# Where the modulation's products are computed: a third of layer 0 moves from TensorE to VectorE, ScalarE and GpSimd, layer 1's loads move to GpSimd's queue

## The chip, the cores and the metric

The kernel runs on one core of a Trainium2 chip. A core has a tensor engine (PE, with its weight loads listed apart as PEld), VectorE (DVE), ScalarE (ACT), GpSimd (POOL) and SyncE (SP), each with an instruction stream of its own that it executes in order. An engine waits for another through semaphores. SP, ACT and POOL can issue DMA transfers; the page lists SP's and ACT's transfers as hardware queues and POOL's as a software queue (q0). The metric is the device time of one execution in microseconds.

## What is computed

Two transformer blocks follow each other on 256 tokens of width 1024, all in fp32. The first block has a gated delta rule, a dilated attention, an output product and a SwiGLU FFN with a short convolution. The second block has two layers with attention and a mixture of 16 experts, and both layers are modulated by a vector c. The change concerns only the modulation:

```python
silu_c = jax.nn.silu(c)
for i in range(DEPTH_2):                       # 2 layers
    mod = silu_c @ ada_w[i] + ada_b[i]         # 1024 x 6144 each
    sh1, sc1, g1, sh2, sc2, g2 = [m[:, None, :] for m in jnp.split(mod, 6, axis=-1)]
    h = rms_norm(x, norm_mix_g[i]) * (1.0 + sc1) + sh1
    ...                                        # attention, y
    x = x + g1 * y
    h = rms_norm(x, norm_ffn_g[i]) * (1.0 + sc2) + sh2
    x = x + g2 * grouped_moe(h, ...)
```

The modulation depends on c and its weights alone, so it can be computed at any time before the second block.

## The kernel before

The first block runs to about 412 us, the second from there to the end. In the first block PE multiplies weights and activations that are each split into a high and a low part (names ending in h and l): ACT makes the high part of a weight block (wh, or whl for both parts in one tile), DVE, sometimes POOL, the low part (wl). `subs` does this for the blocks of one 1 MB load, `feat` multiplies them into features (L572), and lines L588 to L590 into tokens. The FFN has 22 steps (NFF); each has two `feat` blocks, a gate on ACT and DVE (L1109 to L1113), and the product back (L1096 to L1098) for the step before.

The modulation's two weight matrices are 48 MB. The kernel handles them as 48 units of 1 MB, in order, `ada_unit(n)`: units 0 to 23 are layer 0, 24 to 47 layer 1. `ada(n)` adds to a due count and issues the units that are due. It is called by `fill`, which the delta rule and the attention call where PE would wait, and once in each FFN step with a constant `step`; the due counts are the same before and after. Each unit loads a tile `wa` (128 x 2048); there are two such tiles, so a load waits until the unit two before has been read.

- Layer 0, `ada_rows(s, k)`: the tile is a block of 128 rows (k) by 2048 columns (s). PE multiplies it by one column of silu(c), spread over 32 columns: four products of 128 x 512 go to four strips of 32 rows of one PSUM tile (L401). After eight blocks (k = 7) the gate columns get their bias by products with the identity (L409), ACT copies the row out (`adarow`, L412) and sends it to DRAM (`adar`).
- Layer 1: a tile holds four blocks of 128 rows for one slice of 512 columns, and two units (u = 0, 1) make a slice. DVE scales the first block into `acc` (L382) and adds six others by SCALAR_TENSOR_TENSOR (STT, L387), with these exceptions: blocks 3 and 7 are scaled by ACT in place (L384) and added by POOL (L385). `ada_sum` then adds up the 128 partitions of `acc` by products with ones on PE (L422) and, for gate columns, the bias (L425). It runs two slices later.

All loads of both kinds are issued by SP (L396 and L375), in one queue with the weights of the first block. The values come back from `adar` by POOL's loads `adat` and `g`, which also issues the attention tables (`nb`, `rel`, `reld`). The second norm of the first block stands between the output product (`w_out`) and the FFN: ACT squares, POOL takes the root (`rs`, L500), DVE scales (`xn`, L502), PE transposes (L510), ACT and DVE split the result into `hh` and `hl`; some products whose results are not used (L470) run on PE meanwhile. A scheduler of the tile framework arranges each engine's instructions from the order in which the code is written.

The kernel begins with five products of ones (L268), which nothing uses.

Of the kernel before, what the change touches and what calls it, by code (L numbers as in the profile page):

```python
# [13 lines left out]
AF = mybir.ActivationFunctionType  # L14
ALU = mybir.AluOpType
# [78 lines left out]
def _pack(inp):  # L94
    g = {k: np.asarray(v) for k, v in inp.items()}
    A = np.ascontiguousarray

    def cols(v):
        return np.asarray(v).reshape(-1, 128).T

    def feat(w):

        n = w.shape[1]
        return A(w.reshape(KD, 128, n // 256, 2, 128).transpose(2, 1, 3, 0, 4)).reshape(n // 256, 128, 2048)

    def tok(w):

        n = w.shape[1]
        return A(w.reshape(2, 4, 128, n // 512, 512).transpose(3, 0, 2, 1, 4)).reshape(n // 256, 128, 2048)

    o = {"x": A(g["x"][0])}
    prm = np.zeros((128, NPRM), np.float32)
    for name, v in (("ln1", cols(g["ln1"][0])), ("ln2", cols(g["ln2"][0])),
                    ("conv", g["conv_qkv"][0].reshape(4, 12, 128).transpose(2, 1, 0).reshape(128, 48)),
                    ("fconv", g["ffn_conv"][0].reshape(3, 22, 128).transpose(2, 1, 0).reshape(128, 66)),
                    ("gdn", cols(g["gdn_norm"][0])), ("nmix", cols(g["norm_mix_g_2"])),
                    ("nffn", cols(g["norm_ffn_g_2"])), ("c", cols(g["c_2"][0])),
                    ("aqg", np.tile(g["a_q_gain_2"][0], 2)[:, None]), ("akg", np.tile(g["a_k_gain_2"][0], 2)[:, None]),
                    ("asub", g["a_subln_g_2"][0][:, None]),
                    ("bqg", np.tile(g["b_q_gain_2"][0], 2)[:, None]), ("bkg", np.tile(g["b_k_gain_2"][0], 2)[:, None]),  # L120
                    ("adab", cols(g["ada_b_2"]))):
        prm[:, PRM[name][0]:PRM[name][1]] = v
    o["prm"] = prm
    o["row"] = np.concatenate([g["a_log"][0], g["dt_bias"][0], g["router_bias_2"],
                               g["a_lambda_2"][0].ravel()])[None].astype(np.float32)
    o["lnf"] = A(g["ln_f"][None])
    w = g["w_in"][0]
    o["w_qkv"] = feat(w[:, 0:1536])
    o["w_z"] = tok(w[:, 1536:2048])
    o["w_qk"] = feat(w[:, 2056:3080])  # L130
    o["w_v"] = tok(w[:, 3080:3592])
    o["w_ba"] = A(w[:, 2048:2056].reshape(8, 128, 8).transpose(1, 0, 2)).reshape(128, 64)
    o["w_out"] = tok(g["w_out"][0])
    gu = np.stack([g["w_gate"][0].reshape(D, NFF, 128), g["w_up"][0].reshape(D, NFF, 128)], axis=2)
    o["w_gu"] = feat(gu.reshape(D, 2 * NFF * 128))
    o["w_dn"] = A(g["w_down"][0].reshape(11, 2, 128, D).transpose(0, 2, 1, 3)).reshape(11, 128, 2048)

    o["ada_p"] = A(g["ada_w_2"][0].reshape(8, 128, 3, 2048).transpose(2, 0, 1, 3)).reshape(24, 128, 2048)
    o["ada_w"] = A(g["ada_w_2"][1].reshape(2, 4, 128, 12, 512).transpose(3, 0, 2, 1, 4)).reshape(24, 128, 2048)
    o["t5"] = A(g["t5_bias_2"])  # L140
    for p in "ab":
        o[p + "_qkv"] = tok(g[p + "_w_qkv_2"][0])
        o[p + "_wo"] = tok(g[p + "_w_o_2"][0])
    o["rel"] = A(np.pad(g["b_rel_bias_2"][0], ((0, 0), (0, 127)))[:, 383::-1])
    rw = np.zeros((128, 8, 32), np.float32)
    rw[:, :, :16] = g["router_w_2"].reshape(8, 128, 16).transpose(1, 0, 2)
    o["rw"] = rw.reshape(128, 256)
    gu = np.empty((2, 8, 8, 128, 2, 2, 512), np.float32)
    for i, n in enumerate(("moe_w_gate_2", "moe_w_up_2")):
        gu[:, :, :, :, :, i] = g[n].reshape(2, 8, 2, 8, 128, 512).transpose(0, 1, 3, 4, 2, 5)  # L150
    o["m_gu"] = gu.reshape(16, 8, 128, 2048)
    md = g["moe_w_down_2"].reshape(2, 8, 2, 4, 128, D)
    md = md.reshape(2, 8, 2, 2, 2, 128, 2, 512).transpose(0, 1, 6, 3, 5, 2, 4, 7)
    o["m_dn"] = A(md).reshape(16, 4, 128, 2048)
    o["cst"], o["dil"], o["hot"] = _constants()
    return o
# [14 lines left out]
def tile_block(ctx: ExitStack, tc: tile.TileContext, a: dict, out: bass.AP, dbg=None):  # L171
    nc = tc.nc
# [6 lines left out]
    pa = ctx.enter_context(tc.tile_pool(name="pa", bufs=4, space=PSUM))  # L179
# [3 lines left out]
    mm = nc.tensor.matmul  # L183
    V, G, A_ = nc.vector, nc.gpsimd, nc.scalar
# [14 lines left out]
    def w2(shape, name, dt=F32):  # L199
        return act.tile([128] + shape, dt, tag="w2", name=name, bufs=10)  # L200
# [7 lines left out]
    def ps(n=512, tag="pb"):  # L208
        p = pa if tag == "pa" else pb
        return p.tile([128, n], F32, tag=tag, name=tag)  # L210
# [53 lines left out]
    ones = const.tile([128, 128], F32, name="ones")  # L264
    V.memset(ones, 1.0)

    for _ in range(5):
        mm(ps(512, "pa"), ones, ones[:, 0:1].to_broadcast([128, 512]), start=True, stop=True)  # L268
    mhalf = const.tile([128, 8], F32, name="mhalf")
    G.memset(mhalf, -0.5)  # L270
    epsc = const.tile([128, 1], F32, name="epsc")
# [92 lines left out]

    csil = const.tile([128, 8], F32, name="csil")
    adar = [dr.tile([6 * D], F32, name=f"adar{l}") for l in range(2)]
    ada_acc, ada_sums = [None], []

    def ada_unit(n):

        if n < 24:
            return ada_rows(n // 8, n % 8)
        l, s, u = n // 24, n // 2 % 12, n % 2
        w = adap.tile([128, 2048], F32, tag="wa", name="wa", bufs=2)
        nc.sync.dma_start(w, a["ada_w"][n - 24])  # L375
        if u == 0:
            ada_acc[0] = adap.tile([128, 512], F32, tag="acc", name="acc", bufs=3)
        acc = ada_acc[0]
        for i in range(4):
            wi, k = w[:, i * 512:(i + 1) * 512], 4 * u + i  # L380
            if k == 0:
                V.tensor_scalar(acc, wi, csil[:, k:k + 1], None, op0=ALU.mult)  # L382
            elif i == 3:
                A_.activation(wi, wi, AF.Copy, scale=csil[:, k:k + 1])  # L384
                G.tensor_tensor(acc, acc, wi, op=ALU.add)  # L385
            else:
                V.scalar_tensor_tensor(acc, wi, csil[:, k:k + 1], acc, op0=ALU.mult, op1=ALU.add)  # L387
        if u == 1:
            if len(ada_sums) == 2:
                ada_sums.pop(0)()  # L390
            ada_sums.append(lambda: ada_sum(l, s, acc))

    def ada_rows(s, k):

        w = adap.tile([128, 2048], F32, tag="wa", name="wa", bufs=2)
        nc.sync.dma_start(w, a["ada_p"][8 * s + k])  # L396
        if k == 0:
            ada_acc[0] = ps(512, "pa")
        p = ada_acc[0]
        for j in range(4):  # L400
            mm(p[32 * j:32 * j + 32, :], csil[:, k:k + 1].to_broadcast([128, 32]), w[:, j * 512:(j + 1) * 512],  # L401
               start=(k == 0), stop=(k == KD - 1 and (4 * s + j) // 2 not in (2, 5)))
        if k < KD - 1:
            return
        for c in range(4):
            for j in range(4):
                if (4 * s + j) // 2 in (2, 5):
                    n = 16 * s + 4 * j + c
                    mm(p[32 * j:32 * j + 32, c * 128:(c + 1) * 128], P("adab")[:, n:n + 1].to_broadcast([128, 32]), ident,  # L409
                       start=False, stop=(c == 3))  # L410
# [349 lines left out]
    n = 0  # L760
# [64 lines left out]
    for u in range(6):  # L825
        for j, (wh, wl) in enumerate(subs(a["w_qkv"][u] if u else first_)):
            f = 2 * u + j
            p = ps(256, "pa")
            feat(p, hh, wh, wl)
            o = qkvT[f // 4][:, f % 4]  # L830
# [915 lines left out]
```

## Time and profile before

| | us |
|---|---|
| median of 3 runs | 1127.56 |
| lowest, highest | 1124.36, 1133.11 |
| the profiled execution | 1134.06 |
| its span, first to last instruction | 1132.4 |
| PE busy | 1084.4 (96%) |
| DVE busy | 588.6 (52%) |
| ACT busy | 444.1 (39%) |
| POOL busy | 151.8 (13%) |

The shares are averages over stages that have different limits, so the rows below cut the span into stretches. A profile shows one execution: how an engine was busy, what ended each idle time ("idle before, <- releaser"), and when a transfer was issued. When a transfer landed is seen from what began after it.

### The profile page before, as it was taken

What the parts mean: (1) busy time and instruction counts of PE and PEld (TensorE: products, weight loads), DVE (VectorE), ACT (ScalarE), POOL (GpSimd) and SP (SyncE); (2) the same over time, 40 slices, a digit from 0 to 9 for tenths busy, and PEclk for the clock granted to TensorE, in tenths of its full rate; (3) what the DMA queues carried; (4) which work ended last, traced back from release to release, by engine and by line L of the source; (5) the groups of instructions that cost most, each with busy time, mean ns of one, the idle gap of its engine ahead of it and who ended that gap; (6) DMA issues with size and microseconds to landing.
All of it is one profiled execution on the core that took longest, in us unless ns stands there. A gap on an engine that the chain in (4) does not pass through costs nothing. (4 is left out here: it accounts for less than half of the span.)

```text
span 1132.4 us, 16818 instructions
## 1 busy us (share of the span) xinstructions
PE 1084.4 (96%) x6524; PEld 702.4 (62%) x6524; DVE 588.6 (52%) x1215; ACT 444.1 (39%) x901; POOL 151.8 (13%) x126
## 2 busy tenths in 40 slices
PE   8999999999999989999999999898999999999898
PEld 6967666799998868778434343435887634443432
DVE  6954345798998766677412121226667722221212
ACT  5752254655554556667211011216555511110200
POOL 1223112131322241101000000004121000000000
PEclk9999999999999999999999999999999999999999
DMA  8586769878887855455999899999665699989995
GB/s 334 222 290 240 274 243 292 301 262 331 302 338 258 333 227 181 149 179 194 348 401 404 331 424 418 420 420 403 194 197 183 221 406 368 424 337 420 421 422 242
DMA packets 56463, 349.71 MB, mean 309 GB/s; under 512 B 6740, under 2 KB 7492, under 8 KB 19512
## 3 DMA queue, kind: packets, MB, share of 16 engines
q1 hardware_dynamic: 53744, 342.51, 78.0%
q0 software_dynamic: 1792, 5.62, 1.9%
q8 instruction: 54, 0.88, 0.3%
q10 hardware_dynamic: 840, 0.43, 0.1%
q14 instruction: 33, 0.27, 0.1%
HBM read 347.40 MB, written 1.14 MB: 308 GB/s over the span
## 5 line engine op out<-in xcount | busy, mean ns | idle before, releaser
L234 ACT CAST wh<-w 128x1024 fp32r<-128x1024 f32 x132 | 137.6, 1043 | 95.6 <-PE pa L589 67.3
L234 DVE TENSOR_TENSOR wl<-w,wh 128x1024 fp32r<-128x1024 f32 x110 | 136.4, 1242 | 59.3 <-ACT wh L234 46.3
L1578 PE MATMUL pb<-w,XT 128*64 128x512 f32 x672 | 151.8, 595 | 3.7 <-ACTq L1538 3.7
L1578 PEld LDWEIGHTS pb<-w,XT 128*64 128x64 f32 x672 | 47.7, 137 | 91.1 <-issue 81.9
L588 PE MATMUL pa<-wh,hh 128*128 128x512 f32 x224 | 91.0, 408 | 2.5 <-ACT hh L561 2.5
L589 PE MATMUL pa<-wh,hl 128*128 128x512 f32 x224 | 89.2, 398 | 3.0 <-POOL hl L559 1.7
L1597 DVE TENSOR_TENSOR he<-he,pb 128x512 f32<-128x512 f32 (+1 forms) x20 | 11.4, 580 | 154.0 <-PE pb L1578 100.0
L590 PE MATMUL pa<-wl,hh 128*128 128x512 f32 x224 | 88.9, 397 | 0.0
L234 POOL TENSOR_TENSOR wl<-w,wh 128x1024 fp32r<-128x1024 f32 x22 | 53.0, 2407 | 247.6 <-ACT wh L234 206.3
L1615 PE MATMUL pb<-w,heT 128*64 128x512 f32 x352 | 81.0, 603 | 1.5 <-ACT heT L224 1.5
L1596 ACT ACTIVATE he<-pb 128x512 f32<-128x512 f32 (+1 forms) x20 | 10.1, 513 | 184.2 <-PE pb L1578 184.2
L1578 PE MATMUL pb<-wx,XT 128*64 128x512 f32 x352 | 80.2, 595 | 0.0
L1618 DVE SCALAR_TENSOR_TENSOR he<-pb,gsl,g 128x512 f32<-128x512 f32 x32 | 24.1, 752 | 100.3 <-PE pb L1615 100.2
L572 PE MATMUL pb<-hh,whl 128*128 128x256 f32 x320 | 61.9, 286 | 0.0
L234 ACT CAST yh<-he 128x512 fp32r<-128x512 f32 x30 | 18.5, 616 | 107.0 <-DVE he L1618 107.0
L385 POOL TENSOR_TENSOR acc<-acc,wa 128x512 f32<-128x512 f32 x24 | 40.8, 1699 | 134.0 <-DVE acc L387 74.0
L1615 PEld LDWEIGHTS pb<-w,heT 128*64 128x64 f32 x352 | 24.6, 140 | 49.7 <-issue 45.8
L1578 PEld LDWEIGHTS pb<-wx,XT 128*64 128x64 f32 x352 | 25.9, 137 | 46.4 <-issue 45.4
L572 PE MATMUL pb<-hh,wh 128*128 128x256 f32 x192 | 54.4, 284 | 0.0
L572 PE MATMUL pb<-hl,wh 128*128 128x256 f32 x192 | 54.3, 283 | 0.0
L572 PE MATMUL pb<-hh,wl 128*128 128x256 f32 x192 | 54.3, 283 | 0.0
L572 PEld LDWEIGHTS pb<-hh,whl 128*128 128x128 f32 x320 | 51.2, 191 | 2.4 <-issue 1.4
(450 smaller groups left out, 2340.9 us busy)
## 6 DMA issues: line engine op xcount, KB each, us to landing
w<-in_m_gu SPq DMA_DIRECT2D x84, 1024.0 KB
w<-in_m_dn SPq DMA_DIRECT2D x42, 1024.0 KB
wa<-in_ada_p SPq DMA_DIRECT2D x24, 1024.0 KB
wa<-in_ada_w SPq DMA_DIRECT2D x24, 1024.0 KB
wx<-in_m_gu SPq DMA_DIRECT2D x48, 512.0 KB
w<-in_w_gu SPq DMA_DIRECT2D x22, 1024.0 KB
wx<-in_m_gu SPq DMA_DIRECT2D x20, 1024.0 KB
w<-in_a_qkv SPq DMA_DIRECT2D x12, 1024.0 KB
```

The source lines that it names most:

```text
L234: return A_.copy(h, i), (eng or V).tensor_tensor(l, i, h.bitcast(F32), op=ALU.subtract)
L385: G.tensor_tensor(acc, acc, wi, op=ALU.add)
L572: mm(p, w[:, c], r[:, k, :], start=(n == 0), stop=(n == 3 * KD - 1))
L588: mm(p[b], hh_, wh[:, c], start=(k == k0), stop=False)
L589: mm(p[b], hl_, wh[:, c], start=False, stop=False)
L590: mm(p[b], hh_, wl[:, c], start=False, stop=((k + 1) % KD == k0))
L1578: mm(pu[i][64 * e:64 * e + 64, :], xt[k // 4][:, k % 4, c0 + 64 * e:c0 + 64 * e + 64], w(e, i), start=(k == 0), stop=(k == KD - 1))
L1596: A_.activation(he[:, cs], pu[0][:, cs], AF.Silu)
L1597: V.tensor_tensor(he[:, cs], he[:, cs], pu[1][:, cs], op=ALU.mult)
L1615: pin(mm(pd[h][64 * e:64 * e + 64, :], heT[:, k, e, :], w(e, i), start=(k == 0), stop=(k == 3)))
L1618: V.scalar_tensor_tensor(he, pd[h], gsl, g2[:, h * 512:(h + 1) * 512], op0=ALU.mult, op1=ALU.mult)
```

## The change

Layer 0's units with n % 3 == 2 (8 of 24, their columns are 4096 to 6143) go the way of layer 1, through SP's queue; the other 16 stay with `ada_rows`. The arrays are cut accordingly (`ada_p` 16 tiles, `ada_w` 32). Layer 1's loads are issued by POOL (`nc.gpsimd`). In the way of layer 1, block 0 is scaled into `acc` by ACT, blocks 1 to 6 are added by DVE, and block 7 is scaled by ACT into a tile `last` of its own, which POOL adds: one POOL add for each slice where there were two, and DVE has six STT where it had a scaling and five STT. The products at the start are 12 of 216 columns. Lines behind the change stand five further down (L422 becomes L427).

```diff
-    for _ in range(5):
-        mm(ps(512, "pa"), ones, ones[:, 0:1].to_broadcast([128, 512]), start=True, stop=True)
+    for _ in range(12):
+        mm(ps(216, "pa"), ones, ones[:, 0:1].to_broadcast([128, 216]), start=True, stop=True)
...
+        if n < 24 and n % 3 < 2:
+            n = n // 3 * 2 + n % 3
+            return ada_rows(n // 8, n % 8)
         if n < 24:
-            return ada_rows(n // 8, n % 8)
+            n = 16 + n // 3
         l, s, u = n // 24, n // 2 % 12, n % 2
         w = adap.tile([128, 2048], F32, tag="wa", name="wa", bufs=2)
-        nc.sync.dma_start(w, a["ada_w"][n - 24])
+        (nc.gpsimd if l else nc.sync).dma_start(w, a["ada_w"][n - 16])
...
             if k == 0:
-                V.tensor_scalar(acc, wi, csil[:, k:k + 1], None, op0=ALU.mult)
-            elif i == 3:
-                A_.activation(wi, wi, AF.Copy, scale=csil[:, k:k + 1])
-                G.tensor_tensor(acc, acc, wi, op=ALU.add)
+                A_.activation(acc, wi, AF.Copy, scale=csil[:, k:k + 1])
+            elif k == 7:
+                last = w2([512], "last")
+                A_.activation(last, wi, AF.Copy, scale=csil[:, k:k + 1])
+                G.tensor_tensor(acc, acc, last, op=ALU.add)
             else:
                 V.scalar_tensor_tensor(acc, wi, csil[:, k:k + 1], acc, op0=ALU.mult, op1=ALU.add)
...
         if k == 0:
-            ada_acc[0] = ps(512, "pa")
-        p = ada_acc[0]
+            ada_pacc[0] = ps(512, "pa")
+        p = ada_pacc[0]
```

PE before, from the end of the output product (L590) over the second norm to the FFN's first products (L572); `wa,csil` are the modulation's products, `ident,prm` the gate bias, `ident,x` the unused products, `ident,xn` the transposes:

```order
L590 MATMUL pa<-wl,yh 128x512
L401 MATMUL pa<-wa,csil 32x512
L470 MATMUL pa<-ident,x 16x384 x4
L510 MATMUL pb<-ident,xn 128x128 x16
L401 MATMUL pa<-wa,csil 32x512 x7
L409 MATMUL pa<-ident,prm 32x128 x8
L572 MATMUL pb<-hh,wh 128x256
```

PE with the change, in the same place:

```order
L595 MATMUL pa<-wl,yh 128x512
L406 MATMUL pa<-wa,csil 32x512 x3
L414 MATMUL pa<-ident,prm 32x128
L475 MATMUL pa<-ident,x 16x384 x4
L414 MATMUL pa<-ident,prm 32x128 x7
L515 MATMUL pb<-ident,xn 128x128 x16
L577 MATMUL pb<-hh,wh 128x256
```

The products behind the transposes now stand ahead of them; 22 units of four products stood ahead of this place before, 15 and a quarter do now.

POOL before, from the second norm (`rs`) into the FFN:

```order
L234 TENSOR_TENSOR wl<-w,wh 128x1024
L500 TENSOR_TENSOR rs<-rs,mhalf 128x1 x2
L234 TENSOR_TENSOR wl<-w,wh 128x1024
L385 TENSOR_TENSOR acc<-acc,wa 128x512 x3
L1126 DMA rel<-in_rel 16x384
```

POOL with the change, in the same place:

```order
L235 TENSOR_TENSOR wl<-w,wh 128x1024
L379 DMA wa<-in_ada_w 128x2048
L505 TENSOR_TENSOR rs<-rs,mhalf 128x1 x2
L235 TENSOR_TENSOR wl<-w,wh 128x1024
L390 TENSOR_TENSOR acc<-acc,last 128x512
L379 DMA wa<-in_ada_w 128x2048
L466 DMA g_4170<-adar_124 128x1024
L379 DMA wa<-in_ada_w 128x2048
L1131 DMA rel<-in_rel 16x384
L390 TENSOR_TENSOR acc<-acc,last 128x512
L379 DMA wa<-in_ada_w 128x2048
```

The loads of layer 1, 24 in all, now stand between POOL's other work, the first of them ahead of the norm's `rs`; SP's order has none of them any more.

DVE with the change, in the middle of the FFN, with the tiles' numbers: wa_2898 is the tile of the unit two before that of wa_3011, and the two share their place:

```order
L392 SCALAR_TENSOR_TENSOR acc_2812<-wa_2898,csil_123,acc_2812 128x512
L235 TENSOR_TENSOR wl_3061<-w_3031,wh_3060 128x1024
L392 SCALAR_TENSOR_TENSOR acc_3006<-wa_3004,csil_123,acc_3006 128x512 x2
L1116 SCALAR_TENSOR_TENSOR gate_2973<-pb_2914,prm_81,gate_2973 128x255
L392 SCALAR_TENSOR_TENSOR acc_3006<-wa_3004,csil_123,acc_3006 128x512
L1116 SCALAR_TENSOR_TENSOR gate_2973<-pb_2914,prm_81,gate_2973 128x254
L235 TENSOR_TENSOR whl_3121<-w_3119,whl_3121 128x1024
L1118 TENSOR_TENSOR gate_2973<-gate_2973,pb_2915 128x256
L392 SCALAR_TENSOR_TENSOR acc_3006<-wa_3011,csil_123,acc_3006 128x512
```

Between the last reading of a tile and the first reading of the tile that takes its place stand eight instructions here. Layer 1's first STT comes in the fourth FFN step, where before its first scaling came in the first or second.

## Rows read from the trace of the kernel before

**Rows 1.** Stretches: us, busy PE PEld DVE ACT POOL, PEclk, DMA share, GB/s.
```profile
58.00:204.00 146.00, 142.13 (x1272) 100.37 (x1272) 71.12 (x173) 59.30 (x124) 31.54 (x25) 0.99 0.77 274
204.00:214.00 10.00, 8.55 (x58) 4.09 (x57) 7.36 (x12) 4.25 (x12) 3.41 (x3) 1.00 0.61 220
214.00:412.00 198.00, 194.68 (x1447) 177.66 (x1446) 169.94 (x230) 108.05 (x170) 46.98 (x31) 1.00 0.84 312
```

**Rows 2.** Waits of PE, 55 to 420 us: us in total, times, longest.
```profile
PE pa L1096 <- ACT mh L234: 2.6, 1, 2.6
PE pb L510 <- DVE xn L502: 1.4, 1, 1.4
PE pb L870 <- ACT sq L868: 1.3, 1, 1.3
```

**Rows 3.** Waits of DVE, 212 to 412 us, those of the modulation.
```profile
DVE acc L387 <- POOL acc L385: 5.9, 5, 1.6
...
DVE acc L382 <- DMA wa<-in_ada_w: 0.2, 1, 0.2
```

**Rows 4.** Instructions on tile wa, whole span: ns min/median/max, first and last start.
```profile
L401 PE MATMUL pa<-wa,csil x192: 592/593/617, 58.0 to 212.3; 128*32 128x512 f32 x192
L387 DVE SCALAR_TENSOR_TENSOR acc<-wa,csil,acc x60: 735/746/1770, 228.4 to 387.4; 128x512 f32<-128x512 f32 x60
...
L384 ACT ACTIVATE wa<-wa,csil x24: 706/723/731, 220.4 to 379.1; 128x512 f32<-128x512 f32 x24
...
L382 DVE TENSOR_SCALAR acc<-wa,csil x12: 471/478/1533, 223.3 to 376.6; 128x512 f32<-128x512 f32 x12
```

**Rows 5.** Timeline of PE around one unit: start us, duration us, instruction, [idle before].
```profile
104.46 1.06 PE L401 MATMUL pa<-wa,csil 128*32 128x512 f32 x8
105.45 0.74 PE L952 MATMUL pb<-Y,os 64*64 64x64 f32 x18
```

**Rows 6.** Timeline of PE, ACT and DVE behind the second norm.
```profile
210.43 2.66 ACT L237 ACTIVATE hh<-pb,prm 128x256 fp32r<-128x256 f32 x7 [5.02 <-PE pb L510]
210.93 1.66 DVE L238 SCALAR_TENSOR_TENSOR hl<-pb,prm,hh 128x256 fp32r<-128x256 f32 x4 [1.04 <-ACT hh L237]
...
210.97 1.92 PE L401 MATMUL pa<-wa,csil 128*32 128x512 f32 x14
...
213.69 0.39 PE L572 MATMUL pb<-hh,wh 128*128 128x256 f32 x1
...
215.71 0.28 PE L572 MATMUL pb<-hl,wh 128*128 128x256 f32 x1
```

**Rows 7.** Timeline of PE: a gated column sum (L422, L425), the next product.
```profile
316.13 0.45 PE L422 MATMUL pb<-acc,ones 128*32 128x128 f32 x8
...
316.73 0.39 PE L572 MATMUL pb<-hh,whl 128*128 128x256 f32 x1
```

**Rows 8.** Timeline of POOL: a load that it issues and what waits for it.
```profile
244.80 0.56 POOL L1126 DMA_DIRECT2D rel<-in_rel  x1
250.00 1.37 POOL L1129 TENSOR_SCALAR rel<-rel 16x384 f32<-16x384 f32 x1 [4.64 <-DMA rel<-in_rel]
```

**Rows 9.** DVE by line, 214 to 412 us: busy us, mean ns, idle before.
```profile
L234 DVE TENSOR_TENSOR whl<-w,whl 128x1024 fp32r<-128x1024 f32 x30 | 42.7, 1422 | 4.8 <-ACT whl L234 4.8
L234 DVE TENSOR_TENSOR wl<-w,wh 128x1024 fp32r<-128x1024 f32 x33 | 41.9, 1273 | 2.4 <-ACT wh L234 2.2
L1111 DVE SCALAR_TENSOR_TENSOR gate<-pb,prm,gate 128x255 f32<-128x255 f32 (+1 forms) x44 | 21.0, 478 | 7.6 <-ACT gate L1109 7.2
```

**Rows 10.** Timelines of SP and ACT: a modulation load and its first reader.
```profile
253.59 0.33 SPq L375 DMA_DIRECT2D wa<-in_ada_w  x1
...
258.66 0.72 ACT L384 ACTIVATE wa<-wa,csil 128x512 f32<-128x512 f32 x1 [1.68 <-DMA wa<-in_ada_w]
```

**Rows 11.** DMA issues of POOL: number, KB each, median us to landing.
```profile
g<-adar POOLq DMA_DIRECT2D x4, 512.0 KB, 4.1
...
nb<-t5d POOLq DMA_DIRECT2D x2, 256.0 KB, 9.6
```

More of the change, by code (lines that the diff above doesn't have):

```diff
@@ L136, in _pack @@
     o["w_dn"] = A(g["w_down"][0].reshape(11, 2, 128, D).transpose(0, 2, 1, 3)).reshape(11, 128, 2048)
-    o["ada_p"] = A(g["ada_w_2"][0].reshape(8, 128, 3, 2048).transpose(2, 0, 1, 3)).reshape(24, 128, 2048)
-    o["ada_w"] = A(g["ada_w_2"][1].reshape(2, 4, 128, 12, 512).transpose(3, 0, 2, 1, 4)).reshape(24, 128, 2048)
+    o["ada_p"] = A(g["ada_w_2"][0][:, :4096].reshape(8, 128, 2, 2048).transpose(2, 0, 1, 3)).reshape(16, 128, 2048)
+    aw = g["ada_w_2"].reshape(2, 2, 4, 128, 12, 512).transpose(0, 4, 1, 3, 2, 5).reshape(48, 128, 2048)
+    o["ada_w"] = A(aw[16:])
     o["t5"] = A(g["t5_bias_2"])
@@ L366, in tile_block @@
     adar = [dr.tile([6 * D], F32, name=f"adar{l}") for l in range(2)]
-    ada_acc, ada_sums = [None], []
+    ada_acc, ada_pacc, ada_sums = [None], [None], []
     def ada_unit(n):
+        if n < 24 and n % 3 < 2:
+            n = n // 3 * 2 + n % 3
+            return ada_rows(n // 8, n % 8)
         if n < 24:
-            return ada_rows(n // 8, n % 8)
+            n = 16 + n // 3
         l, s, u = n // 24, n // 2 % 12, n % 2
         w = adap.tile([128, 2048], F32, tag="wa", name="wa", bufs=2)
-        nc.sync.dma_start(w, a["ada_w"][n - 24])
+        (nc.gpsimd if l else nc.sync).dma_start(w, a["ada_w"][n - 16])
         if u == 0:
```

## The prediction

> **What bounds the kernel now.** I read the stretches first: TensorE (PE) is busy 142.1 of 146 us before the end of the first block's output product, 8.6 of 10 us in the norm behind it, and 194.7 of 198 us in the first block's FFN [rows 1]. So PE is the bound in all the code that the change touches, and what is taken off it there should come off the time, unless something else steps into its place. Second, PE's waits between 55 and 420 us: the longest is 2.6 us in the FFN, then come 1.4 us (for xn) and 1.3 us (for the squares), so there is hardly a hole for removed work to have filled [rows 2]. Third, the neighbour: VectorE (DVE) is busy 71 of 146 us before the norm, but 169.9 of 198 us in the FFN [rows 1]. That is 86%, the second bound, and the FFN is where a wait on DVE can reach PE. Fourth, who waits around the modulation: in the FFN DVE stood 5.9 us behind POOL's adds, and 0.2 us for a load of a modulation tile [rows 3].
>
> The profiled execution took 1134.06 us, of which 1132.4 are its span and 1.7 lie around it; that is 6.5 above the median of the three runs. I sum in the execution's microseconds and take the difference to the median, 1127.56.
>
> **What leaves PE.** A unit is one 1 MB tile: eight records of 593 ns [rows 4]. They are not worth 4.7 us. The unit that starts at 104.46 occupies 1.06 us, and the next product starts 0.99 us after it: the four 32-column products run side by side [rows 5]. I take 0.99 us a unit. Eight of 24 units leave PE. By the order, 22 units stood before the end of the output product and 15.25 do now: 6.75 x 0.99 = 6.7 us. A block of gate rows moves from before that point to behind it: its twin in the norm lies between the last unit's end (210.97 + 1.92 = 212.9) and 213.69 [rows 6], so 0.8. One of the four new column sums comes before that point: a gated sum starts at 316.13 and the next product at 316.73, so 0.6 for a gated one, and for a plain one the 0.45 of its first part at most, 0.4 [rows 7]. At the end of the output product PE is thus ahead by 6.7 + 0.8 - 0.4 = 7.1 us, at most.
>
> **The norm.** Before, 14 of 16 products of two units and a gate block stand between the transposes and the FFN's first product: from 210.97 to 213.69, 2.7 us [rows 6]. Now they stand ahead of the warm products, under the wait for the norm, and the transposes meet the FFN directly. But the FFN's first block needs eight hh from ScalarE (ACT, 2.66 us for seven from 210.43) and eight hl, which now set its pace [rows 6]. Eight hl at 1.66/4 from 210.93 end at 214.3; the first block's last product would follow then. Before, the seventeenth product started at 215.71, 2.02 us after the first, 0.126 each, so the 24 ended at about 216.7 [rows 6]. So between 0 and 2.4 us is won; I take 1.5. Against this, POOL's order now has the load of unit 24 ahead of the two rs of that norm. One issue on POOL is 0.56 us [rows 8]. If its wait (the release of a tile by PE) ends before rs is ready it costs nothing, if not up to 0.6; I take 0.3.
>
> **What DVE and ACT receive before the norm.** 24 STT of 0.746 us (17.9 us) [rows 4] come into the stretch in which DVE is idle for 75 of 146 us [rows 1], and 8 ACT scalings of 0.72. Most hide in idle time (in the FFN, ACT keeps its 24 scalings). Two places don't: an ACT scaling falls among the squares at 64 to 67 us, where PE already waits 1.3 for ACT [rows 2], up to 0.7; and three STT stand between copies of the attention and the delta-rule chain (about 158 to 162 us), where each STT could put 0.75 in front of a short latency chain, up to 2.2. Together 0 to 2.9; I take 1.2, since PE has other products in order there.
>
> So the FFN starts 7.1 + 1.5 - 0.3 - 1.2 = 7.1 us earlier.
>
> **The FFN.** The other three sums of layer 0 (two of them gated) now run here, in a stretch that PE fills: 0.4 + 2 x 0.6 = 1.6 us back. DVE per pair of layer 1: five STT and one scaling before (5 x 0.746 + 0.478 = 4.21), six STT now (4.48); over 12 pairs 3.2 us more. Against it, 24 POOL adds become about 12. An add stretches the DVE instruction beside it: the STT is 0.746 in the median and 1.77 at most, the scaling 0.478 and 1.53 [rows 4]. If each add costs DVE half of that largest stretch, (1.77 - 0.75) / 2 = 0.5 (an estimate), twelve fewer give 6 back, and 3.2 are spent: 2.8 won. The 5.9 us behind adds [rows 3] should at least halve as well. PE, which is the bound, sees little of it; between a loss of 3 and a gain of 3 I take 0 for the sum, because layer 1 begins three or four steps later by the order and the same work is squeezed into fewer steps.
>
> The warm-up goes from 5 x 512 to 12 x 216 columns (2560 to 2592). That is 1% more of the same work. What it can move is the clock: the granted clock is 0.99 on the mean from 58 to 204 us [rows 1], 1.5 us of that stretch, which a changed pattern of work could remove or double. Between -1.5 and +1.5 I take 0.
>
> Sum: -7.1 + 1.6 + 0 = -5.5; I round to -5 for the small holes that a removed filler leaves (waits of the kind of the 1.3 and 1.4 [rows 2]). On the median: 1122.5, say 1123.
>
> **The new wait, and why it decides.** All 24 loads of layer 1 go from SP to POOL, into the software queue. Each waits for its tile's release, each second one behind an add, and they hold up adds, the loads rel, reld and adat and each other. From SP one landed 5.07 us after its issue (253.59 to 258.66) [rows 10]. From POOL no 1 MB load is in the trace. Nearest rows: 24 KB took 5.1 us (244.80 to POOL's start at 250.00), 512 KB 4.1 and a strided 256 KB 9.6 [rows 8, 11]. So 4.1 to 9.6; being nearest in kind and size to the 512 KB rows with twice their bytes, I take 6. What cover is there? Between the last STT on a tile and the first on the tile that replaces it, the order puts in the tight places a whl, a wl, three STT, two long gate instructions and a shorter one (from tile wa_2898 to wa_3011 in the change's rows): 1.42 + 1.27 + 3 x 0.75 + 2 x 0.48 = 5.9 us [rows 4, 9], with the shorter one (some 0.4) 6.3. An issue of 0.56 and, for even units, an ACT scaling of 0.72 must fit too. So a landing of over 5.0 us (even) or 5.7 (odd) makes DVE wait, and DVE executes in order: the splits whl and wl of the FFN weights stand behind it, and PE waits for those. With 6 us it waits 0.6 us on the mean, some 18 times, 11 us in all, against 198 - 170 = 28 us in which DVE was idle [rows 1]: hidden.
>
> The Trainium skill ("DMA: Bandwidth & Descriptors", section "Anatomy of one DMA") gives about 2.0 us plus bytes / 436 GB/s for this path, 4.4 us for 1 MB: by it no wait at all, and the sum would stand. No row of before shows it; the 24 KB load of 5.1 us [rows 8] speaks against it.
>
> **Rivals.**
> - *Relief given back (1127 to 1130).* PE arrives 7 us earlier at an FFN that DVE then paces, with layer 1's work in fewer steps. For it: 86% DVE. Against: DVE has some 3 us less to do. Gives -1 to +2.
> - *The loads come late (slower).* Place: layer 1's loads from step 3 or 4 on. Price: a landing of 8 us is 2.6 us a unit over some 18 tight units, 47 us, less the 28 us of idle time: +19, less the 5 won: +14, about 1141. It turns to slower from 5.4 + 33 / 18 = 7.2 us a landing and passes 1% at 5.4 + 44 / 18 = 7.8 (5.4 being the middle of the two limits above). For it: 9.6 us for 256 KB [rows 11], and the weights' 312 GB/s beside it [rows 1]. Against: 4.1 us for 512 KB [rows 11]. The Trainium skill ("SBUF — State Buffer", section "SBUF: two separate sides") says that descriptors of POOL's loads can't be written while DVE runs certain two-port copies, and gives 3.1 us in place of 0.62; in this trace an issue on POOL took 0.56 us [rows 8], which neither proves nor refutes it.
> - *All of it pays (1116).* -7.1 with none of the 1.2 and 0.3 lost is -8.6; with 3 us on DVE and 1.5 from the clock, less 1.6 for the sums, -10 to -13.
> - *It changes nothing on PE.* If the units lay in PE's holes. PE's waits are too short for that [rows 2]; it falls under the first rival.
>
> **Numbers.** Forecast (-8 to -2) 0.45; relief given back 0.25; late loads 0.18; all pays 0.12. 1% is 11.3 us, about what a measurement of this kernel can tell from no change. Faster by it: most of the last case, 0.10. Slower: two thirds of the late loads, 0.13. The rest, 0.77, is within 1%. The range cuts half of each outer case: 1113 to 1137.
>
> **What would show it.** The end of the output product 6 us earlier, the FFN's first product near 213.7 - 7.1 = 206.6 and the FFN's end 4 to 6 us earlier. Right on the loads: DVE's waits for a modulation load below 15 us in all. Wrong: those waits above 30 us, or PE waiting for whl and wl; then the landing rows of the software queue will read above 7 us. If the end of the output product comes less than 4 us earlier, the step on latency chains is wrong; if the FFN alone grows without DVE waits, the step on DVE's load.

## The result, and the profile after

The changed kernel is 1.0% slower: 1141.17 us median against 1129.35 for the kernel before, ratio 1.010 with a 95% interval of 1.0067 to 1.0133. The forecast was 1123 us (range 1113 to 1137); the change missed it on the side of the rival that the prediction called "the loads come late". The profiled execution of the changed kernel took 1142.02 us, 1140.4 of them its span.

Three starts of products on PE divide the time: the last product of the output product, the FFN's first product, and the FFN's last product. With the profile before they were 203.53, 213.69 and, in PE's timeline:

```profile
412.45 0.39 PE L1098 MATMUL pa<-wl,mh 128*128 128x512 f32 x1
```

With the change the first is at 195.44, and the other two are:

```profile
205.38 0.39 PE L577 MATMUL pb<-hh,wh 128*128 128x256 f32 x1 [1.61 <-DVE hl L239]
...
416.72 0.39 PE L1103 MATMUL pa<-wl,mh 128*128 128x512 f32 x1
```

So the FFN starts 8.3 us earlier and ends 4.3 us later: it takes 211.3 us where it took 198.8, and 12.6 us are lost there. The stretches that answer [rows 1] (same columns):

```profile
58.00:204.00 146.00, 139.77 (x1256) 100.59 (x1254) 92.37 (x202) 65.54 (x137) 39.43 (x31) 1.00 0.80 288
204.00:214.00 10.00, 8.62 (x71) 8.62 (x72) 8.84 (x15) 9.01 (x14) 0.00 (x0) 1.00 0.34 125
214.00:412.00 198.00, 188.64 (x1399) 169.01 (x1398) 160.52 (x218) 101.51 (x164) 42.90 (x43) 0.98 0.82 300
```

In the FFN PE is busy 6 us less than in [rows 1] in the same 198 us, DVE 9 us less. Who waits in the FFN (205 to 420 us; us in total, times, longest), first DVE, then PE:

```profile
DVE acc L392 <- DMA wa<-in_ada_w: 18.3, 7, 3.8
DVE acc L392 <- ACT acc L386: 5.2, 3, 3.1
```

```profile
PE pa L1102 <- DVE ml L235: 6.2, 5, 2.4
PE pa L1101 <- ACT mh L235: 2.0, 2, 1.6
PE pb L577 <- DVE hl L239: 1.6, 1, 1.6
PE pb L427 <- POOL acc L390: 1.1, 1, 1.1
```

DVE waits 18.3 us for a modulation tile itself, and 5.2 us more for ACT's scaling of a block, which waited for its tile: 23.5 us where [rows 3] had 0.2. ACT itself waits no longer than before: 26.9 us for modulation tiles, where it waited 26.4. PE waits for ml and mh, the two parts of the FFN's gated features. Its 1.6 us for hl lie ahead of the FFN's first product, so in the FFN it waits 9.3 us.

The loads of layer 1 (a load has landed when its data are there to be read), from the view of tile wa and from the list of DMA issues (ns min/median/max; then us from issue to landing min/median/max; then the list's medians):

```profile
L379 POOL DMA_DIRECT2D wa<-in_ada_w x24: 537/577/607, 197.1 to 382.2; - x24
DMA to landing us min/median/max: 5.2/7.0/9.1
```

```profile
wa<-in_ada_w POOLq DMA_DIRECT2D x24, 1024.0 KB, 7.0
...
g<-adar POOLq DMA_DIRECT2D x4, 512.0 KB, 4.6
...
rel<-in_rel POOLq DMA_DIRECT2D x1, 24.0 KB, 7.7
```

7.0 us is the number that the prediction lacked and put at 6; the SP load of [rows 10] took 5.07. One place shows the whole chain, from the issue to PE (timelines of SP, POOL, DVE and PE):

```profile
310.22 2.19 SPq L290 DMA_DIRECT2D w<-in_w_dn  x2
...
313.18 0.58 POOL L379 DMA_DIRECT2D wa<-in_ada_w  x1
...
321.54 0.75 DVE L392 SCALAR_TENSOR_TENSOR acc<-wa,csil,acc 128x512 f32<-128x512 f32 x1 [3.85 <-DMA wa<-in_ada_w]
322.21 0.42 DVE L235 TENSOR_TENSOR ml<-gate,mh 128x256 fp32r<-128x256 f32 x1
...
322.69 0.50 PE L1102 MATMUL pa<-wh,ml 128*128 128x512 f32 x1 [2.42 <-DVE ml L235]
```

Two weight loads of 1 MB have been issued by SP, 3.0 and 1.1 us before POOL issues the tile at 313.18. DVE can use it 8.4 us later, having waited 3.85 us. Right behind the waiting STT in DVE's order stands ml, and PE waits 2.42 us for that. Six of the seven waits of 18.3 us have ml right behind them: behind waits of 2.05, 3.76, 1.19, 3.85, 2.16 and 2.96 us, PE waited 0, 1.79, 0, 2.42, 0.56 and 0 us for that ml.

Behind such waits the clock falls (stretches of 4 us; the third value from the end is the granted clock):

```profile
280.00:284.00 4.00, 2.21 (x8) 1.69 (x8) 3.19 (x5) 2.46 (x5) 0.00 (x0) 0.90 0.51 209
284.00:288.00 4.00, 4.00 (x21) 3.55 (x20) 4.00 (x5) 1.38 (x3) 2.63 (x2) 0.67 0.85 274
...
320.00:324.00 4.00, 1.58 (x8) 1.10 (x7) 2.46 (x4) 1.82 (x3) 0.00 (x0) 1.00 0.61 254
324.00:328.00 4.00, 4.00 (x17) 3.47 (x16) 3.96 (x5) 2.97 (x4) 2.62 (x2) 0.57 0.60 199
```

PE was busy 2.21 and 1.58 of 4 us, and after that it ran at the lower of its levels for a while: (0.10 + 0.33) x 4 = 1.7 us are lost by the one fall, and 0.43 x 4 = 1.7 by the other. The FFN of [rows 1] was granted 1.00.

The 12.6 us of the FFN can now be added up. Four views of the FFN alone, from its first product to the end of its last: of before, of the change, and of two runs that are described below and in which PE waits for nothing there, e4 (before, with the new scaling) and e5 (the change with its loads on SP and the old first products):

```profile
213.69:412.84 199.15, 195.82 (x1451) 178.34 (x1449) 171.09 (x231) 108.52 (x171) 47.82 (x31) 1.00 0.84 312
```

```profile
205.38:417.11 211.73, 202.37 (x1489) 181.53 (x1489) 170.88 (x233) 110.68 (x177) 44.13 (x44) 0.98 0.80 291
```

```profile
210.19:404.87 194.68, 194.67 (x1451) 178.30 (x1449) 168.06 (x231) 110.34 (x171) 27.49 (x19) 1.00 0.86 319
```

```profile
203.91:400.75 196.84, 196.84 (x1489) 179.01 (x1489) 170.69 (x233) 111.72 (x177) 28.88 (x21) 1.00 0.84 317
```

PE is idle for 9.4 us where it was idle for 3.3: 6.0 of the 12.6 us are additional waits. The other 6.6 are longer busy time: 3.4 by the two falls of the clock, 2.2 by the three moved sums (e5 against e4, which have the change's 1489 and the 1451 products of before at a clock of 1.00), and 1.0 that these rows do not assign. Behind the FFN the changed kernel's profile is 3.7 us longer than that of before, with the same number of PE records; in stretches of 4 us the clock takes 10.2 us there, where it took 6.8.

The clock counts for more over all executions than in this one. Each execution's mean granted clock is on record. The 23 of the kernel before that ran beside e1 took 1124.0 to 1133.9 us at clocks of 0.989 to 0.997; less (1 - clock) x 1132 us, an estimate of what the clock took, they lie between 1119.4 and 1122.9. The four of the change had 0.986 to 0.990 and lie between 1126.2 and 1129.2. By this estimate about half of what the change loses is a lower clock.

### The profile page after: what moved, and what is told of

The parts are those of the page before. It is cut to its first block, busy times and chain, and to the rows that moved or that the text cites. A ratio compares the mean times of both kernels' runs of the same rounds, so it can differ in the third digit from the quotient of the medians.

```text
span 1140.4 us, 16816 instructions
## 1 busy us (share of the span) xinstructions
PE 1083.0 (95%) x6506; PEld 709.1 (62%) x6506; DVE 604.1 (53%) x1239; ACT 450.1 (39%) x912; POOL 153.0 (13%) x142
## 5 line engine op out<-in xcount | busy, mean ns | idle before, releaser
L392 DVE SCALAR_TENSOR_TENSOR acc<-wa,csil,acc 128x512 f32<-128x512 f32 x96 | 75.6, 787 | 24.5 <-DMA wa<-in_ada_w 18.3
L1601 ACT ACTIVATE he<-pb 128x512 f32<-128x512 f32 (+1 forms) x20 | 10.1, 513 | 185.2 <-PE pb L1583 185.2
```

The costliest lines, as they stand in the source:

```text
L1601: A_.activation(he[:, cs], pu[0][:, cs], AF.Silu)
```

## The experiments

Ratios are to the kernel before, measured beside it on the same chip. "FFN" is from its first to the start of its last product in the profiled execution; before it was 198.8 us, with the change 211.3.

| run | edit | ratio (95%) | FFN starts | FFN |
|---|---|---|---|---|
| the change | | 1.010 (1.0067 to 1.0133) | 205.4 | 211.3 |
| e1_sp | change, layer 1's loads on SP | 0.9959 (0.9941 to 0.9976) | 206.9 | 196.7 |
| e2_b_pool | before, layer 1's loads on POOL | 1.0339 (1.0304 to 1.0374) | 210.7 | 237.7 |
| e3_third_only | before, a third of layer 0 moved | 1.0098 (1.0066 to 1.0129) | 204.1 | 204.8 |
| e4_arith_only | before, new scaling | 0.9981 (0.9960 to 1.0002) | 210.2 | 194.3 |
| e5_warm_old_sp | e1 with the old first products | 0.9971 (0.9949 to 0.9994) | 203.9 | 196.5 |
| e6_noadd_pool | change, no POOL adds in layer 1 | 1.0051 (1.0024 to 1.0078) | 207.0 | 205.7 |
| e7_noadd_sp | e6 with the loads on SP | 0.9971 (0.9945 to 0.9998) | 203.7 | 196.5 |
| e8_even_pool | change, only u = 0 on POOL | 0.9997 (0.9970 to 1.0023) | 208.9 | 200.6 |
| e9_odd_pool | change, only u = 1 on POOL | 1.0110 (1.0073 to 1.0148) | 203.6 | 214.9 |
| e10_act | change, layer 1's loads on ACT | 1.0246 (1.0215 to 1.0277) | 207.2 | 225.2 |
| e11_sp_inplace | e1, block 7 scaled in place | 0.9946 (0.9921 to 0.9972) | 205.0 | 196.9 |
| e12_load_first | change, POOL's adds behind the loads | 1.0085 (1.0056 to 1.0115) | 206.7 | 212.2 |

The scheduler arranges DVE's order anew when a load changes its engine, so any two of these runs can differ in that order too; the waits below are read from each run's own trace. In the FFN, by a count of what matches, 226 of the change's 233 DVE instructions stand in the same sequence in e12, 214 in e9, 206 in e1 and 158 in e8. No run sets this order apart from the queue.

### The queue alone, undone and alone

```diff
-        (nc.gpsimd if l else nc.sync).dma_start(w, a["ada_w"][n - 16])
+        nc.sync.dma_start(w, a["ada_w"][n - 16])
```

> The changed kernel with layer 1's loads issued by SP again, nothing else undone. Theory (late loads: from POOL they land 7.0 us after their issue, DVE waits 24 us for them and the FFN grows by 12.6 us): the FFN falls from 211.3 to 199 to 203 us, DVE's waits for a modulation load fall below 3 us, and the time is 1141 - 9 to 12, so 1129 to 1132, or lower if the relief on PE holds (8 us at the FFN's start): down to 1122. Rival (DVE has more to do in fewer steps, loads beside the point): the FFN stays above 207 us and the time above 1137.

Measured: 1122.71 us, FFN 196.7. DVE's and ACT's waits for these loads (200 to 420 us):

```profile
DVE acc L392 <- DMA wa<-in_ada_w: 0.5, 2, 0.3
```

```profile
ACT acc L386 <- DMA wa<-in_ada_w: 0.8, 1, 0.8
```

One line of the change turns 1.010 into 0.996, and PE waits for nothing in this FFN. DVE is as busy there as with the change (170.0 and 170.9 us), so the rival (DVE's work paces the FFN) falls. The other direction, on the kernel before:

```diff
-        nc.sync.dma_start(w, a["ada_w"][n - 24])
+        nc.gpsimd.dma_start(w, a["ada_w"][n - 24])
```

> The kernel before with layer 1's loads issued by POOL and nothing else changed. Theory (late loads): landing 7 us, DVE and ACT wait over 15 us for modulation loads in the FFN, FFN from 198.7 to 207 to 212 us, time 8 to 13 us above before. Rival (DVE's work): FFN within 2 us of before, time within 3 us.

Measured: 1166.1 us, a loss of 3.4% or 38 us, where 8 to 13 were expected. DVE and ACT (200 to 420 us), then PE:

```profile
DVE acc L387 <- DMA wa<-in_ada_w: 15.4, 5, 6.4
```

```profile
ACT wa L384 <- DMA wa<-in_ada_w: 70.6, 18, 8.7
```

```profile
PE pa L1096 <- ACT mh L234: 14.4, 4, 6.9
```

The mechanism is the same, but in the old scaling ACT scales blocks 3 and 7 and meets the load first: it waits 70.6 us (26.4 in the kernel before), with the casts of the weights and mh behind it in its order, and PE waits 14.4 us for mh. The theory expected a size of 8 to 13 us because it counted DVE alone.

### The other parts one by one

```diff
-                V.tensor_scalar(acc, wi, csil[:, k:k + 1], None, op0=ALU.mult)
-            elif i == 3:
-                A_.activation(wi, wi, AF.Copy, scale=csil[:, k:k + 1])
-                G.tensor_tensor(acc, acc, wi, op=ALU.add)
+                A_.activation(acc, wi, AF.Copy, scale=csil[:, k:k + 1])
+            elif k == 7:
+                last = w2([512], "last")
+                A_.activation(last, wi, AF.Copy, scale=csil[:, k:k + 1])
+                G.tensor_tensor(acc, acc, last, op=ALU.add)
```

> The kernel before with the new scaling alone (block 0 by ACT, blocks 1 to 6 by DVE, block 7 by ACT and POOL). Theory: DVE gains the stretching of 12 POOL adds and loses 3 us of STT; time within 3 us of before. Rival (the six STT or the wait of the first STT for ACT lengthen the FFN): 3 to 8 us above before.

Measured: 0.9981, an interval that just reaches 1. So what the scaling is worth is between a gain of 0.4% and nothing. In the one trace the FFN takes 194.3 us, 4.5 less than in the one trace before. One step of it is visible: before, PE waited 2.56 us for mh at 370.04, behind a whl on DVE that took 2.30 us (364.94) beside a POOL add (364.86); with one add for each slice this wait is gone.

The third of layer 0 alone (the loads on SP, the old scaling and the old first products; the edit is the changed rule of `ada_unit` without the queue):

> Only the third of layer 0 moves from PE: the loads stay with SP, the first products stay 5 x 512, and the order of scaling and adding stays that of before (block 0 on DVE, blocks 3 and 7 on ACT and POOL). Theory (late loads are the only loss): FFN starts 7 to 8 us earlier and takes 199 to 202 us, time 4 to 7 us below before. Rival (layer 1 begins later, so DVE paces the FFN): FFN starts as early but takes 205 us or more, time within 2 us of before or above it.

Measured: 1.0098. The FFN starts 9.6 us earlier than in the profile before and takes 204.8 us. So with the old scaling the moved third costs more than it gains, as the rival expected. Its reason (layer 1 has fewer steps, DVE paces the FFN) is not shown: PE waits again for mh (2.5 us) and for a gate (2.3 us), ACT 36.1 us for its tiles, but the FFN still ends 3.6 us earlier than in the profile before, and the profiled execution is the fastest of the six. What is on record for all six is the clock: 0.987 on the median, against 0.995 for the 23 executions before, by the estimate above 9 of the 11 us. What lowers it is open. With the new scaling the third costs nothing, as the next run shows.

```diff
-    for _ in range(12):
-        mm(ps(216, "pa"), ones, ones[:, 0:1].to_broadcast([128, 216]), start=True, stop=True)
+    for _ in range(5):
+        mm(ps(512, "pa"), ones, ones[:, 0:1].to_broadcast([128, 512]), start=True, stop=True)
```

> The changed kernel with layer 1's loads on SP and the first products of before (5 x 512): third of layer 0 moved and new scaling, nothing else. Theory (the 12 narrow first products are worth nothing): within 2 us of the same kernel with the narrow ones (ratio 0.996 to before). Rival (they move the clock's first fall at 12 to 20 us or later ones): 2 to 4 us above it, ratio 0.998 to 1.0, and one fall of the granted clock more in the trace.

Measured (on e1): 0.9971 against 0.9959; the intervals overlap, so the first products are worth nothing that these runs can tell. Beside e4 (0.9981) the third of layer 0 gains nothing that can be told either, though in the traces e5's FFN starts 6.3 us earlier (203.9 against 210.2) and ends 4.1 us earlier.

### Why POOL's loads come late

Two things put a load from POOL behind one from SP. POOL adds the last block first, so the second load of each slice is issued 1.3 to 2.4 us after the last reading of its tile (the first load 0.6; 0.1 on SP in e1); and the landing itself takes longer. Four runs and a later pair separate them. First without POOL adds:

```diff
-            elif k == 7:
+            elif k == 7 and not l:
```

> The changed kernel, but layer 1's last blocks are added by VectorE (a seventh STT) and POOL adds nothing there: in the FFN it only issues loads, so no load stands behind an add. Theory A (the loss is the loads' place behind POOL's adds, which put every second issue 1.5 to 2.4 us after the release): at most 4 us above the same kernel with SP's loads (next run). Theory B (the loss is the landing in the software queue, 7 us against 5): release to issue 0.6 us throughout, landing still about 7, and 10 to 18 us above the next run. Both in equal parts: 5 to 9.

> The same as the run before with layer 1's loads on SP: its control. DVE has 12 more STT (9 us) and no POOL add beside it. If DVE's work paced the FFN here it takes 5 to 9 us more than with the adds on POOL (1122.7); if the loads alone decide, within 3 us of it.

Measured: 1.0051 and 0.9971, so 0.8%, 9 us, remain without any add on POOL. The waits of DVE in e6, and of PE:

```profile
DVE acc L392 <- DMA wa<-in_ada_w: 10.0, 5, 4.7
DVE acc L392 <- ACT acc L386: 5.1, 4, 2.5
```

```profile
PE pa L1101 <- ACT mh L235: 4.9, 1, 4.9
```

The landing is 7.5 us on the median. ACT also waits for these loads, 28.7 us in all and up to 7.2, and the 4.9 us of PE come behind that wait of ACT. The second expectation (DVE's work) came out within 3 us, as the loads alone decide. Then half the loads:

```diff
-        (nc.gpsimd if l else nc.sync).dma_start(w, a["ada_w"][n - 16])
+        (nc.gpsimd if l and u == 0 else nc.sync).dma_start(w, a["ada_w"][n - 16])
```

(and `u == 1` in the other run)

> The changed kernel with only the first load of each slice (u = 0, 12 of 24) on POOL, the others on SP. Theory A (place behind the adds): these are the loads that were issued 0.6 us after the release, so the loss of 18 us nearly goes: within 4 us of the kernel with all loads on SP (1122.7). Theory B (landing): half of it stays, 6 to 10 us above. Theory C (two loads of the one software queue delay each other): landing falls to 5.2 to 6 us and the loss to under 5.

> The changed kernel with only the second load of each slice (u = 1) on POOL. Theory A (place behind the adds): these loads came 1.5 to 2.4 us after the release, so most of the 18 us stays: 10 us or more above 1122.7. Theory B (landing): 6 to 10 us, as with the first loads. Theory C (loads of the one queue delay each other): under 5.

Measured: 0.9997 and 1.0110. Against e1 the first loads cost 0.4%, the second loads all of it (e8's DVE order differs most from the change's, so the 0.4% is less sure). In e9 DVE waits:

```profile
DVE acc L392 <- DMA wa<-in_ada_w: 26.8, 9, 6.2
```

Landing, from the lists of issues of e8 and e9:

```profile
wa<-in_ada_w POOLq DMA_DIRECT2D x12, 1024.0 KB, 5.4
```

```profile
wa<-in_ada_w POOLq DMA_DIRECT2D x12, 1024.0 KB, 7.5
```

Theory C (the two loads of the software queue delay each other) falls by e9: alone in the queue, its loads land in 7.5 us. What they meet is SP's weights. Four of the 12 landed in 5.2 to 5.5 us; the last load that SP had issued before them lay 2.8 us or more back. The other eight were issued 1.0 to 1.4 us behind a weight load of SP and took 7.0 to 10.4 us. The wait of e9 that cost PE most (timelines of SP, POOL, DVE and PE):

```profile
311.03 2.21 SPq L290 DMA_DIRECT2D w<-in_w_dn  x2
...
313.98 0.54 POOL L379 DMA_DIRECT2D wa<-in_ada_w  x1
...
324.11 0.75 DVE L392 SCALAR_TENSOR_TENSOR acc<-wa,csil,acc 128x512 f32<-128x512 f32 x1 [5.61 <-DMA wa<-in_ada_w]
...
325.25 0.80 PE L1102 MATMUL pa<-wh,ml 128*128 128x512 f32 x1 [4.74 <-DVE ml L235]
```

2.95 and 1.1 us before the load, SP has issued a weight load; the tile is there after 10.1 us, and nearly the whole wait of DVE goes over to PE.

From SP single loads land as late, but most do not. In the FFN before, ACT's 13 waits for a modulation tile ([rows 10] has one of them) tell 13 landings: 4.9 to 8.2 us after the issue, 5.1 on the median. In e11, whose loads are all on SP, 18 are told in the same way, 4.8 to 8.6 with a median of 5.2; with the change 14, 6.3 to 9.1 with a median of 7.6. And the loads that share the time with a second queue come later on both sides. Counted from the packets in the traces, given to the issues of a queue in their order, the last packet of the 11 loads that stay on SP in e9's FFN ends 6.7 us after the issue on the median, that of the 23 in e1's FFN 4.7 (a landing follows some 0.4 us later where both are known).

Is it the place behind the adds after all? The same place in SP's queue, and the other order on POOL:

```diff
-                last = w2([512], "last")
-                A_.activation(last, wi, AF.Copy, scale=csil[:, k:k + 1])
-                G.tensor_tensor(acc, acc, last, op=ALU.add)
+                A_.activation(wi, wi, AF.Copy, scale=csil[:, k:k + 1])
+                G.tensor_tensor(acc, acc, wi, op=ALU.add)
```

> The changed kernel with layer 1's loads on SP, and block 7 scaled in place in the tile (as before) in place of a tile of its own, so that POOL's add releases the tile: every second load must be issued after the add, 1.3 us or more later, but in SP's queue. Theory A (the place behind the adds costs by itself): some 12 issues 1.5 to 2.5 us late, 3 to 8 us above the kernel with a tile of its own (ratio 0.996), so 0.999 to 1.003. Theory B (only the landing in the second queue costs): within 2 us of it, ratio 0.995 to 0.998.

> The changed kernel, loads on POOL as in the change, but each add of POOL is issued behind the load of the same release, so that no load waits for an add. Theory A (place behind the adds): release to issue falls to 0.6 us for all units, and about a third to a half of the loss of 16 us goes (the run without POOL's adds was 1.005): ratio 1.002 to 1.006. Theory B (landing alone): as the change, 1.008 to 1.012.

Measured: 0.9946 and 1.0085. Theory A falls twice. On SP a load that has to wait for the add costs nothing: e11 has the lowest ratio measured here (its interval overlaps e1's), though each second load is issued 1.5 to 4.9 us after the last reading of its tile, behind the add, and DVE waits 10.2 us in it (200 to 420 us), in short pieces:

```profile
DVE acc L391 <- DMA wa<-in_ada_w: 6.1, 4, 1.9
DVE acc L391 <- ACT acc L386: 4.1, 4, 1.7
```

On POOL, with each load ahead of the add (issued 0.3 to 0.6 us after the last reading but for one, 1.4), the time stays nearly that of the change, and DVE's waits too:

```profile
DVE acc L403 <- DMA wa<-in_ada_w: 11.6, 6, 3.7
DVE acc L403 <- ACT acc L394: 10.8, 4, 4.8
```

```profile
PE pa L1112 <- ACT mh L235: 6.5, 3, 3.4
PE pa L1113 <- DVE ml L235: 3.1, 4, 1.6
```

So the landing in the second queue is the larger part; the place behind the adds is 0.15% by e12, within the noise, and at most the difference between e6 and the change, 0.5%, and e6 differs by an STT in place of each add.

A hardware queue next to SP's, on ACT:

```diff
-        (nc.gpsimd if l else nc.sync).dma_start(w, a["ada_w"][n - 16])
+        (nc.scalar if l else nc.sync).dma_start(w, a["ada_w"][n - 16])
```

> The changed kernel with layer 1's loads issued by ACT into a hardware queue of its own, so that they are neither behind POOL's adds nor in the software queue, but also no longer in one row with the weights on SP. Theory S (the software queue lands late by itself): landing 5 to 5.5 us, DVE's waits for these loads under 8 us, time within 4 us of SP's (ratio 0.996 to 1.0), unless ACT's own order holds them up. Theory W (any second queue shares the transfer engines with the weights that are under way): landing 7 us as from POOL, DVE's waits 10 to 20 us, ratio 1.003 to 1.01.

Measured: 1.0246. It tells the two theories not apart. The issues now stand in ACT's order behind casts and gates and came 2.5 us after the release on the median of the 22 later loads (up to 8.2); that may be enough for the waits:

```profile
DVE acc L392 <- ACT acc L386: 14.0, 6, 3.2
DVE acc L392 <- DMA wa<-in_ada_w: 8.4, 5, 2.4
```

By the packets of ACT's queue the last one of a load ended 5.7 us after the issue on the median (23 loads, 4.5 to 8.9), later than e1's 4.7. So it stays open what a second hardware queue that is issued in time would cost. That sharing with the weights makes POOL's landing late is argued from rows (e9's eight behind weight loads and four without, and SP's own loads in e9), not isolated by a run.

## Why the prediction was wrong

- **What leaves PE: right.** Predicted: 7.1 us less 1.2 at the end of the output product, so 5.9. Measured against the profile before 8.1, of which 1.8 are the clock: the profile before has falls at 12 to 20 and at 152 to 160 us (3.4 us in all), the change's only the first (1.7). That leaves 6.3. e4 and e5, which have no fall there, end this product at 200.0 and 194.8, 5.2 apart.
- **The norm: right in size.** From the last product of the output product to the FFN's first product it was 10.2 us before, 9.9 with the change, and 9.1 in e5, where POOL has no load ahead of rs. The prediction had 1.5 won and 0.3 lost to POOL's load; it was 1.0 won, 0.8 of it lost: the first rs starts 1.5 us after the start of that last product in e5, and 2.3 us after it with the change, right behind the issue of the load.
- **The FFN's work: wrong in sign.** The sum put it at 0 with the sums on top. By single profiles the new scaling gains 4.5 us of the FFN (e4; the ratio of its runs tells a gain of 0 to 4.5 us in the whole), the three sums cost 2.2 and not 1.6, and e1 and e5 take 196.7 and 196.5 us, 2.1 to 2.3 less than before.
- **The new wait: this is the step that failed.** Its landing was put at 6 us, nearest to the 512 KB rows with their median of 4.1 [rows 11]. It measured 7.0 (7.7 for the 24 KB load). The median hid the one of the four that was issued in the first block (its rows stand below: POOL's timeline, then the lists of issues from 175.5 to 190 us and from 500 to 900 us). The load of 10.5 us stood behind four nb loads of its own queue, in a stretch that moved 278 GB/s; the three of 4.1 ran in stretches of 117 to 131 GB/s. The loads of the change run in the FFN, which moves 312 GB/s [rows 1]. The place of each second load behind an add, which the prediction named, got no price in its cover: 0.56 us stood for an issue that came 1.3 to 2.4 us after the last reading. By e12 that mattered little.

```profile
176.05 0.57 POOL L461 DMA_DIRECT2D g<-adar  x1
g<-adar POOLq DMA_DIRECT2D x1, 512.0 KB, 10.5
...
g<-adar POOLq DMA_DIRECT2D x3, 512.0 KB, 4.1
```

- **And its cover.** The prediction let 28 us of DVE's idle time absorb the waits, as a total. By this the rival's point of turning was 7.2 us and the measured 7.0 would have been free. The runs show that a total is the wrong measure: e11 has 10.2 us of waits, none over 1.9, and PE waits 0.3 us in its FFN; e6 has 15.1, one of 4.7, and its FFN takes 9.2 us more than e7's; the change has 23.5, up to 3.85, and pays 6.0 us more in PE's waits. The waits of the same place tell what counts: the length of each one against what DVE is ahead with the instruction behind it. At 321.54 a wait of 3.85 cost PE 2.42, so 1.4 us were covered; in e9 5.61 cost 4.74, 0.9 covered; at 390.68 a wait of 2.96 cost PE nothing for ml.
- **The queued instruction: half right.** The prediction named the splits whl and wl as what PE would wait for. It waits for ml, which stands behind the STT in DVE's order, and for mh on ACT; in e10 it waits for whl, wl and wh, 14.5 us.
- **The clock: not counted as a price of waiting.** The prediction gave the clock up to 1.5 us by chance. Two falls in the FFN, each behind a wait of PE, cost 3.4, and over the four executions the lower clock is about half of the loss, by the estimate above.
- **The rival that happened** was named with the right place and the right direction (18%, about 1141 us). Its price was worked out for 8 us a landing and came out by a different path: 7.0 us, fewer microseconds of wait than assumed (23.5 against 47), less cover than assumed, and the clock. That its 1141 us is the measured time is luck. Its sign fell in between: 23.5 us of waits lie above the 15 that would have been right on the loads and below the 30 that would have been wrong.

The Trainium skill's "DMA: Bandwidth & Descriptors" ("Anatomy of one DMA") has a fit from which 4.4 us for 1 MB on this path is worked out, an estimate. Not one of the 24 loads was so early: the shortest took 5.2 us, the median 7.0, the longest 9.1. The same page of the Trainium skill has 6.15 us for 1 MB in its table of measurements ("Bandwidth"), without the issue; that lies nearer. The Trainium skill's "SBUF — State Buffer" ("SBUF: two separate sides") would put a delay down to VectorE holding a port against the writing of descriptors. These traces give it no support: POOL's issues take 0.54 to 0.61 us throughout, as before; in the 3.5 us behind an issue of e9 DVE is as busy for a load that lands in 5.2 us (3.50 at 287.06) as for one that takes 10.1 (3.46 at 313.98); and the late landings go with weight loads.

## What to carry over

Moving a prefetch to another engine's queue is not free because the bytes are the same: here it gave up its place in the row of the other loads, and landed later where it ran beside them. Work out the landing from loads that ran beside the same traffic, and the cover from the instruction that stands behind the waiting one, not from the engine's idle total. And test a change's parts apart: here one line held the whole loss, and without it the rest is 0.3 to 0.5% faster than before (e1, e5, e11).

## What the runs showed of the hardware

A 1 MB load from POOL landed 5.2 to 9.1 us after its issue with the change and 5.2 to 11.5 in e2; from SP 4.9 to 8.2 (median 5.1, the 13 loads of the kernel before that ACT waited for in the FFN). In e9 the eight loads issued 1.0 to 1.4 us behind a weight load took 7.0 to 10.4 us, the four others 5.2 to 5.5. In the change's FFN the granted clock fell behind two waits of PE, of 1.79 and 2.42 us, and each fall cost about 1.7 us. The falls differ from execution to execution of a like program: up to the output product the profile of before has two and that of e4 none, which makes 3.4 us where no edit had come into play yet. Over the 23 executions of the kernel before, the estimate from the mean granted clock accounts for most of the 10 us between the fastest and the slowest; so two single profiles can differ by several microseconds with nothing changed there, and the ratio over several runs is the measure.
